# Thirty-two bytes less padding in front of the working tiles of a two-layer encoder

## The chip, the cores and the metric

The kernel runs on one core of one Trainium2 chip. It is one launch. The metric is the device time of one execution, in microseconds; the time of a kernel is the median of its runs. The core has a matrix engine (PE, with its weight loads shown apart as PEld), a vector engine (DVE), an activation engine (ACT), GpSimd (POOL) and a queue engine (SP) that issues most of the transfers. All of them work on SBUF, 128 partitions of on-chip memory; a tile takes the same byte addresses in each partition, so "address" below means the byte within a partition.

## The reference, cut to what matters

A trunk of two layers on x of 512 tokens by 1024 features, all in float32:

```
for l in range(2):
    h = rmsnorm(x, attn_norm[l])
    proj = h @ w_in[l]                       # 1024 -> 3072
    sb_out = stick_breaking_attention(...)   # 8 heads of 64
    df_out = differential_attention(...)     # 4 heads, two maps of 64 each, then a norm
    x = x + concat(sb_out, df_out) @ w_o[l]  # 1024 -> 1024
    h = rmsnorm(x, mlp_norm[l])
    u = square(relu(h @ w_ff1[l]))           # 1024 -> 4096
    x = x + u @ w_ff2[l]                     # 4096 -> 1024
return rmsnorm(x, final_norm)
```

## The kernel before, in words

**Three products for one.** Every large matrix product is made from operands split in two: a value is rounded to the type float32r (the "hi" part, by ACT in L109 or L233), and the rest is the value minus that (the "lo" part, by DVE in L125 or L234). The helper `three` (L284 to L289) then issues three matmuls into the same accumulator: hi by hi (L287), then the first operand's hi by the second's lo (L288), then lo by hi (L289). Two of three in a row use the same stationary operand. A matmul has a *stationary* operand (128 by 128, loaded into the array by a weight load) and a *moving* operand (up to 512 columns that stream past it). In profile rows the names stand as `out<-moving,stationary`.

**The stages of a layer.** First come the projections. The query and key blocks (outputs named `p`, with a head name such as `p0s1q`) have a weight block as the stationary operand (`whi`, `wlo`) and the 512 tokens of the normalised input as the moving one (`h_hi`, `h_lo`). The value blocks (`p0u`, `p0w` and so on, L427 to L429) are the other way round: 128 tokens of `h_hi` or `h_lo` are stationary and 256 columns of weights move. Attention (scores `S`, transposes `T`, values `O`) is interleaved by hand with the projections and with the first half of the output projection (`wo<-mdh`, `wo<-mdl`). The second half of it (`wo<-vdh`, `wo<-vdl`) runs alone. Then the MLP runs in four groups. Each has eight blocks `f` of 24 matmuls (stationary `whi`/`wlo`, moving `h_hi`/`h_lo`), and then 168 matmuls of the second MLP product in chains `X`, `V` and `Y`, which use seven products where eight would be plain; there the split activations `Ah`/`Al` are stationary and the weights `whi`/`wlo` move, 512 columns at a time.

**What sets the order.** Each engine executes its instructions in the order written out; `behind` adds ordering edges, and a small planner with a running clock decides between which projection steps an attention step is put. Weights arrive by transfer in `raw` tiles (SP queue) or `q` tiles (SP, and POOL for the ones added in the transfer), are split into `whi`/`wlo`, and are used by PE one or two units later.

**Where tiles lie.** Tiles take SBUF in the order in which pools and tiles are declared, each rounded up to 32 bytes. The pool `cp` (opened in L165) is first, behind 2,176 bytes that the program reserves. It holds, in this order: `lead` (a tile that nothing reads, 128 bytes), `begin`, `x`, `h_hi`, `h_lo`, `ssq`, `rbc`, `cos_t`, `sin_t`, `edge`, then small constants of 4 to 96 bytes (`lam_sm` to `fin`), and last `trail` (L230), a tile that nothing reads. Behind `cp` come the pools for `raw`, for `whi`/`wlo`, and all the pools of attention and of the MLP (`md*`, `v*`, `x*`, `z*`, `st*`, `kl*`, `hl*`, `y*`, `q*`, `F`, `Ah`, `Al`). All of these start one after another, and are multiples of 512 bytes long, but for a few small ones and the tiles `C` at the end of the attention pools.

So `x` begins at byte 3,072, which is 6 times 512; `h_hi` at 19,456, `h_lo` at 35,840, and `ssq` to `edge` at 52,224 to 60,416: all multiples of 512. `raw` begins at byte 63,008, which is 123 times 512 and 32 more, and so do all large tiles behind it: `whi` at 75,296, `wlo` at 83,488, `mdh` at 91,680, `vdh` at 124,448, the first `Ah` at 140,832, the second pair of `whi` in the MLP at 198,176, each 32 bytes past a multiple of 512. PE reads slices of these tiles at offsets that are multiples of 512 bytes (but for the single columns that `rms_b` spreads), so the remainder of a tile is the remainder of every operand that PE takes from it.

The lines that carry it:

```
    cp.tile([P, 32], F32, tag="lead", name="lead")
    begin = cp.tile([P, 192], F32, tag="begin", name="begin")
...
    fin = cp.tile([P, 24], F32, tag="fin", name="fin")
    cp.tile([P, 32], F32, tag="trail", name="trail")
```

Of the kernel before, what the change touches and what calls it, by code (L numbers as in the profile page):

```python
# [9 lines left out]
F32 = mybir.dt.float32  # L10
# [7 lines left out]
P = 128  # L18
# [144 lines left out]
def trunk(ctx, tc, opened, xT, w, w2, gfin, lamv, cos, sin, out):  # L163
    nc = tc.nc
    cp = ctx.enter_context(tc.tile_pool(name="cp", bufs=1))  # L165
# [61 lines left out]
    mean = cp.tile([P, 4], F32, tag="mean", name="mean")  # L227
    r2 = cp.tile([P, 4], F32, tag="r2", name="r2")
    fin = cp.tile([P, 24], F32, tag="fin", name="fin")
    cp.tile([P, 32], F32, tag="trail", name="trail")  # L230

    def split(hi, lo, src):
        a = nc.scalar.activation(hi, src, AF.Copy)  # L233
# [925 lines left out]
```

## Time and profile before

| | |
|---|---|
| time, median of 3 runs | 1157.63 us (1157.55 to 1157.69) |
| time of the profiled execution | 1158.41 us |
| its span | 1156.5 us |
| PE busy | 1146.8 us, 99% of the span, 5749 matmuls |
| weight loads busy | 964.4 us, 83% |
| DVE, ACT, POOL busy | 811.3, 642.3, 141.2 us |
| transfers | 166.47 MB |

The span is the time from the first instruction to the last; the profiled execution's own time is 1.9 us longer than its span. Matmuls overlap in the records: one of 512 columns is recorded as some 390 ns long, while the next begins some 230 ns after it. So the recorded duration is not what a matmul costs; the distance from one start to the next is. In a stretch in which PE runs without a gap that distance is the length of the stretch divided by the number of matmuls in it.

### The profile page before, as it was taken

How to read it: one execution, taken by the hardware profiler on the slowest of the kernel's cores; microseconds unless marked ns; L12 is line 12 of the kernel's file. 1: busy time of each engine (PE TensorE's matmuls, PEld its weight loads, DVE VectorE, ACT ScalarE, POOL GpSimd, SP SyncE). 2: the span in 40 equal slices, each digit the busy share in tenths (PEclk: the TensorE clock that was granted, in tenths of full speed). 3: DMA queues.
4: the chain of work that ended last, by engine and by line, in shares of the span. 5: the costliest groups of instructions: out<-in, count | busy, mean ns of one | idle time of the engine just before them, and what ended most of it. 6: DMA issues, size and time to landing. Idle time of an engine off the chain costs nothing.

```text
span 1156.5 us, 15843 instructions
## 1 busy us (share of the span) xinstructions
PE 1146.8 (99%) x5749; PEld 964.4 (83%) x5749; DVE 811.3 (70%) x1313; ACT 642.3 (56%) x1147; POOL 141.2 (12%) x225
## 2 busy tenths in 40 slices
PE   9999999999999999999999999999999999999997
PEld 7899889888888888888888998988888888888886
DVE  7898788775645746746778977887657467466476
ACT  6456666656646445455445665765574454553554
POOL 1000333100101101001000013330011010010010
PEclk9999999999999999999999999999999999999999
DMA  7564453266754845835226744522748459358162
GB/s 250 156 196 141 112 158 94 73 210 154 187 176 83 216 141 90 244 120 95 89 73 188 196 110 145 148 72 74 253 93 218 147 91 243 121 93 253 40 122 94
DMA packets 55853, 166.47 MB, mean 144 GB/s; under 512 B 6880, under 2 KB 8160, under 8 KB 55776
## 3 DMA queue, kind: packets, MB, share of 16 engines
q1 hardware_dynamic: 46128, 131.36, 35.8%
q0 software_dynamic: 9216, 33.56, 17.1%
q8 instruction: 45, 0.74, 0.3%
q10 hardware_dynamic: 432, 0.56, 0.1%
q14 instruction: 32, 0.26, 0.1%
HBM read 138.18 MB, written 2.10 MB: 121 GB/s over the span
## 4 chain that ended last, share of the span: by engine, by line
PE 96%; DVE 1%; DMA 1%; ACT 1%; issue 1%; POOL 0%; POOLq 0%; DVEq 0%; ACTq 0%
PE f L287 10%; PE f L288 10%; PE f L289 10%; PE X L287 5%; PE X L288 5%; PE X L289 5%; PE wo L287 3%; PE wo L288 3%; PE wo L289 3%; PE V L287 2%; PE V L289 2%; PE V L288 2%; PE Y L287 1%; PE Y L289 1%; PE Y L288 1%; PE T1s L606 1%
## 5 line engine op out<-in xcount | busy, mean ns | idle before, releaser
L125 DVE TENSOR_TENSOR wlo<-raw,whi 128x1024 fp32r<-128x1024 f32 (+1 forms) x130 | 154.2, 1189 | 113.7 <-ACT whi L109 111.7
L109 ACT ACTIVATE whi<-raw 128x1024 fp32r<-128x1024 f32 (+1 forms) x130 | 131.8, 1018 | 149.0 <-PE f L288 50.0
L287 PE MATMUL f<-h_hi,whi 128*128 128x512 f32 x512 | 202.9, 396 | 0.0
L109 ACT ACTIVATE whi<-q 128x512 fp32r<-128x512 f32 x224 | 129.9, 623 | 131.1 <-PE X L289 44.1
L288 PE MATMUL f<-h_lo,whi 128*128 128x512 f32 x512 | 202.5, 395 | 0.0
L289 PE MATMUL f<-h_hi,wlo 128*128 128x512 f32 x512 | 202.5, 395 | 0.0
L125 DVE TENSOR_TENSOR wlo<-q,whi 128x512 fp32r<-128x512 f32 x224 | 145.3, 687 | 78.6 <-ACT whi L109 74.2
L289 PEld LDWEIGHTS f<-h_hi,wlo 128*128 128x128 f32 x512 | 96.2, 188 | 23.3
L287 PEld LDWEIGHTS f<-h_hi,whi 128*128 128x128 f32 x512 | 96.2, 188 | 23.0
L288 PEld LDWEIGHTS f<-h_lo,whi 128*128 128x128 f32 x512 | 96.2, 188 | 23.0
L234 DVE TENSOR_TENSOR Al<-F,Ah 128x256 fp32r<-128x256 f32 (+2 forms) x96 | 74.7, 779 | 45.8 <-ACT Ah L233 45.8
L287 PE MATMUL X<-whi,Ah 128*128 128x512 f32 x248 | 96.9, 391 | 0.0
L288 PE MATMUL X<-wlo,Ah 128*128 128x512 f32 x248 | 96.6, 389 | 0.0
L289 PE MATMUL X<-whi,Al 128*128 128x512 f32 x248 | 96.5, 389 | 0.0
L233 ACT ACTIVATE Ah<-F 128x256 fp32r<-128x256 f32 (+2 forms) x96 | 67.6, 704 | 49.9 <-DVE F L892 48.1
L856 POOL DMA_DIRECT2D q<-in_w x48 | 41.9, 873 | 434.2 <-DVE wlo L125 386.0
L289 PEld LDWEIGHTS X<-whi,Al 128*128 128x128 f32 x248 | 46.5, 188 | 9.8
L287 PEld LDWEIGHTS X<-whi,Ah 128*128 128x128 f32 x248 | 46.6, 188 | 9.6
L288 PEld LDWEIGHTS X<-wlo,Ah 128*128 128x128 f32 x248 | 46.5, 188 | 9.6
L287 PE MATMUL V<-whi,Ah 128*128 128x512 f32 x128 | 49.8, 389 | 0.0
L288 PE MATMUL V<-wlo,Ah 128*128 128x512 f32 x128 | 49.8, 389 | 0.0
L289 PE MATMUL V<-whi,Al 128*128 128x512 f32 x128 | 49.8, 389 | 0.0
(658 smaller groups left out, 2557.8 us busy)
## 6 DMA issues: line engine op xcount, KB each, us to landing
raw<-in_w SPq DMA_DIRECT2D x126, 512.0 KB, 3.6
q<-in_w SPq DMA_DIRECT2D x64, 512.0 KB, 5.8
q<-in_w POOLq DMA_DIRECT2D x64, 512.0 KB, 5.5
x<-in_xT SPq DMA_DIRECT2D x8, 256.0 KB, 4.6
out_xT<-y SPq DMA_DIRECT2D x6, 256.0 KB, 2.2
raw<-in_w SPq DMA_DIRECT2D x6, 128.0 KB, 4.2
cos_t<-in_cos SPq DMA_DIRECT2D x2, 256.0 KB, 5.0
sin_t<-in_sin SPq DMA_DIRECT2D x2, 256.0 KB, 4.9
```

The costliest lines, as they stand in the source:

```text
L109: return self.nc.scalar.activation(o, src, AF.Copy)
L125: self.last = h, nc.vector.tensor_tensor(out=lo[:, a:b], in0=raw[:, a:b], in1=hi[:, a:b].bitcast(F32), op=ALU.subtract)
L233: a = nc.scalar.activation(hi, src, AF.Copy)
L234: nc.vector.tensor_tensor(out=lo, in0=src, in1=hi.bitcast(F32), op=ALU.subtract)
L287: nc.tensor.matmul(pt, ah, bh, start=first, stop=False, skip_group_check=goes_on)
L288: nc.tensor.matmul(pt, ah, bl, start=False, stop=False, skip_group_check=goes_on)
L289: nc.tensor.matmul(pt, al, bh, start=False, stop=last, skip_group_check=goes_on)
L606: nc.tensor.transpose(pt[:, off : off + P], u["w"][qi][:, kb * P : (kb + 1) * P], ident)
L856: nc.gpsimd.dma_start(t, quad(g, q, c), accum_op=ALU.add)
```

## The change

The pad `trail` at the end of `cp` is 24 floats long in place of 32, that is 96 bytes in place of 128. Nothing in `cp` before it moves. Everything behind it begins 32 bytes earlier: `raw` at 62,976, which is 123 times 512, `whi` at 75,264, and so on. With that, all large tiles begin at multiples of 512 bytes, except the two tiles `C` of the attention (2,052 bytes each), which lie behind small ones and move by the same 32 bytes. No instruction is added, removed or put in another place, on any engine, and no shape changes.

```diff
     fin = cp.tile([P, 24], F32, tag="fin", name="fin")
-    cp.tile([P, 32], F32, tag="trail", name="trail")
+    cp.tile([P, 24], F32, tag="trail", name="trail")
```

## The prediction

> **What bounds the kernel now.** I read the page first, then who PE waited for, then PE's busy time by stretches, and last single starts.
>
> ```profile
> span 1156.5 us, 15843 instructions
> PE 1146.8 (99%) x5749; PEld 964.4 (83%) x5749; DVE 811.3 (70%) x1313; ACT 642.3 (56%) x1147; POOL 141.2 (12%) x225
> PEclk9999999999999999999999999999999999999999
> PE 96%; DVE 1%; DMA 1%; ACT 1%; issue 1%; POOL 0%; POOLq 0%; DVEq 0%; ACTq 0%
> ```
>
> ```profile
> PE warm L217 <- POOL edge L211: 1.4, 1, 1.4
> PE S0s L519 <- DMA kl0s1k<-hl0s1q: 0.5, 1, 0.5
> ```
>
> PE is busy for 99% of the span at the full granted clock, 96% of the chain that ended last is PE, and in the whole execution it waits 1.9 us for others. Nothing that shortens a transfer or another engine can bring more than a few microseconds. The time is the sum of what matmuls cost one after another; the question is whether a matmul costs the same at other addresses.
>
> ```profile
> 0.00:20.00 20.00, 18.57 (x80) 13.64 (x81) 13.42 (x28) 15.94 (x29) 1.44 (x11) 1.00 0.85 292
> 325.00:369.80 44.80, 44.80 (x194) 36.06 (x192) 21.29 (x30) 24.49 (x38) 2.62 (x3) 1.00 0.43 110
> 369.80:407.90 38.10, 38.10 (x169) 31.54 (x168) 29.10 (x43) 18.31 (x29) 4.38 (x5) 1.00 0.80 212
> 580.00:813.00 233.00, 232.89 (x1387) 205.00 (x1385) 189.85 (x332) 138.44 (x286) 40.53 (x73) 1.00 0.44 127
> ```
>
> The columns after a stretch's length are busy time and number of PE, PEld, DVE, ACT and POOL, then clock, DMA share and GB/s. The second stretch is the eight `f` blocks of one MLP group, the third the group's `X`, `V` and `Y`. Both are gapless, with 512 columns per matmul and the same pattern of three. By the weight loads that start in each, 44.80 / 192 = 233.3 ns per matmul, and 38.10 / 168 = 226.8 ns. The same work costs 6.5 ns more in `f`. The starts show that it is steady:
>
> ```profile
> 516.01 0.40 PE L287 MATMUL f<-h_hi,whi 128*128 128x512 f32 x1
> 516.24 0.40 PE L288 MATMUL f<-h_lo,whi 128*128 128x512 f32 x1
> 516.48 0.40 PE L289 MATMUL f<-h_hi,wlo 128*128 128x512 f32 x1
> 516.71 0.40 PE L287 MATMUL f<-h_hi,whi 128*128 128x512 f32 x1
> ...
> 541.08 0.39 PE L287 MATMUL V<-whi,Ah 128*128 128x512 f32 x1
> 541.30 0.39 PE L288 MATMUL V<-wlo,Ah 128*128 128x512 f32 x1
> 541.53 0.39 PE L289 MATMUL V<-whi,Al 128*128 128x512 f32 x1
> 541.76 0.39 PE L287 MATMUL V<-whi,Ah 128*128 128x512 f32 x1
> ```
>
> What differs is which tiles are read. In `f` the moving operand lies at a multiple of 512 bytes and the stationary one 32 bytes past one; I write this (0, 32). In `X`, `V`, `Y` both lie 32 past: (32, 32). The costliest groups by form allow a test, since a recorded duration follows the distance (6 ns between `f` and `X`):
>
> ```profile
> L287 PE MATMUL f<-h_hi,whi 128*128 128x512 f32 x512 | 202.9, 396 | 0.0
> L289 PE MATMUL f<-h_hi,wlo 128*128 128x512 f32 x512 | 202.5, 395 | 0.0
> L288 PE MATMUL X<-wlo,Ah 128*128 128x512 f32 x248 | 96.6, 389 | 0.0
> L289 PE MATMUL V<-whi,Al 128*128 128x512 f32 x128 | 49.8, 389 | 0.0
> L288 PE MATMUL wo<-mdl,whi 128*128 128x512 f32 x64 | 25.2, 393 | 0.0
> L289 PE MATMUL wo<-mdh,wlo 128*128 128x512 f32 x64 | 25.1, 392 | 0.0
> L289 PE MATMUL wo<-vdh,wlo 128*128 128x512 f32 x64 | 24.9, 389 | 0.0
> L289 PE MATMUL Y<-whi,Al 128*128 128x512 f32 x64 | 24.9, 389 | 0.0
> L428 PE MATMUL p0u<-wlo,h_hi 128*128 128x256 f32 x64 | 17.9, 279 | 0.0
> L606 PE MATMUL T0s<-edge,sig0s 128*128 128x128 f32 x80 | 11.3, 272 | 0.0
> L289 PE MATMUL p<-h_hi,wlo 128*128 128x512 f32 x28 | 11.1, 396 | 0.0
> L918 PE MATMUL xT<-edge,x 128*128 128x128 f32 x32 | 4.1, 272 | 0.0
> L630 PE MATMUL O0s<-zl,vs 128*128 128x256 f32 x16 | 4.1, 281 | 0.0
> ```
>
> `wo<-vdh` has the same stationary tiles as `f` (`whi`, `wlo`), but a moving tile at 32: 389, like `X`, not like `f`. So neither the stationary tile nor the stage makes `f` slow; the moving one does, alone or by its distance from the stationary one. `wo<-mdh` is (32, 32) too, but cut up by attention steps: 392 to 393, between the two.
>
> **The change part by part.** It moves every tile behind the pad by 32 bytes: (32, 32) becomes (0, 0), (0, 32) becomes (0, 0), and so does (32, 0), the case of the value projections. No instruction, wait or queue moves. I take the reading that the *difference* of the two remainders counts, because two streams that read one memory side by side meet or miss each other by their distance, and a shift of both alike leaves that as it was. No row shows a 512-column product at (0, 0), so this is a choice, and both ends are kept below.
>
> `f`: 2 layers × 4 groups × 192 = 1536 matmuls (three rows of x512), from 233.3 to 226.8 ns: 1536 × 6.5 = −10.0 us, all on the path, since PE has no gap there. The cover holds: in the `f` stretch DVE and ACT are busy 21.29 and 24.49 us of 44.80, which becomes 43.5.
>
> Query and key projections `p`: 32 units × 24 = 768 matmuls, also (0, 32) now, most of them cut up by attention. Bounds: 0, and 768 × 6.5 = 5.0 us. The nearest row for a cut-up (0, 0) is `wo<-mdh,wlo` with 392 to 393, against 396 for `p`: 3 ns, so 768 × 3 = −2.3 us.
>
> Value projections, 16 units of 48 matmuls with 256 columns, 768 in all: (32, 0) to (0, 0). The last blocks of the kernel have 256 columns at (32, 32):
>
> ```profile
> L288 PE MATMUL Z<-wlo,Ah 128*128 128x256 f32 x4 | 1.1, 283 | 0.0
> ```
>
> 283 against 279 gives 768 × 4 = +3.1 us as one end. The other is half of what 512 columns gain, 768 × 3.3 = −2.5 us, in case they behave alike. The cut-up `O0s<-zl,vs` with 281 lies nearest in kind, as these products too are cut up by attention: 768 × 2 = +1.5 us.
>
> `X`, `V`, `Y`, both halves of `wo`, the scores and `O`: (32, 32) to (0, 0), nothing by this reading. Transposes: `T0s` reads a stationary tile at 32 and `xT` one at 0, both 272 ns: nothing. DVE and ACT could only matter where they are late for PE; in the attention stretch DVE is busy 189.85 of 233 us and PE 232.89, so there is no place where a few ns per instruction would come out. Transfers write other addresses, but PE's waits for them sum to 0.5 us. In the first 20 us PE is idle for 1.43 us and DMA at 0.85; whatever the loads gain there is bounded by that 1.43.
>
> Sum: −10.0 − 2.3 + 1.5 = −10.8 us. Against the profiled execution's own time (1158.41: the span and 1.9 us around it) that gives 1147.6; this execution is 0.8 us above the median of the runs, so for the median 1157.63 − 10.8 = 1146.8 us. This reading's own range: from −10.0 − 5.0 − 2.5 = −17.5 to −10.0 + 3.1 = −6.9, that is 1140 to 1151.
>
> **The rivals.** *A moving operand at a multiple of 512 is slow whatever the stationary one is.* Then `f` and `p` stay, and 744 `X`, 384 `V`, 192 `Y` and 192 `wo<-vdh` matmuls go from 226.8 to 233.3: 1512 × 6.5 = +9.8; 192 cut-up `wo<-mdh` by 3 ns give +0.6, the value projections between 0 and +2.5. It ends at 1168 to 1171 us, slower. For it: each 512-column group with moving 0 is slow and each with 32 fast, without exception. Against it: that 0 should be worse by itself than 32 needs a reason which nothing here shows. It decides from the first (0, 0) product at 233 in `X`.
>
> *Each operand has its own price.* From 256 columns, a stationary operand at 0 saves 4 ns (279 against 283); from 512, a moving one at 0 costs 6.5. Then (0, 0) lies between, at 233.3 − 4 = 229.3: `f` and `p` gain 2304 × 4 = 9.2 us, the 1512 lose 1512 × 2.5 = 3.8, the 192 cut-up some 0.5, and the value projections lose half of 6.5 on 768, 2.5 us. Net −2.4 us, 1155.2, at the edge of no change.
>
> *Addresses do nothing.* Then `f` is slow for another reason, say where `h_hi` and `h_lo` lie in the memory at large, and the time stays at 1157.6. For it speaks that the transposes do not care about 0 or 32. Against: `p` takes its weights only from the tiles at 75,296 and on, `f` also from those at 198,176, and both have 395 to 396; nothing else that I find separates `f` from `wo<-vdh`.
>
> The Trainium skill, page "SBUF — State Buffer", section "Who interferes with whom", gives PE two independent read ports, one for the moving operand and one for weight loads, and says that PE never waits on anyone; by that rule the change does nothing. Two steady rates for the same form at a clock of 1.00 and without a wait are not what the rule leads one to expect, so I give it little.
>
> **How the numbers follow.** A measurement of this kernel tells about 0.2%, 2.3 us, from no change. The distance reading: 0.54, at 1146.8. The moving operand alone: 0.30, at 1168 to 1171. Own prices: 0.08, at 1155.2, on the border, counted half as faster and half as the same. No effect: 0.08. So faster 0.58, same 0.12, slower 0.30. The range goes from 1141 to 1169: it holds the first case but for its lowest end, both middle ones, and the lower part of the slow one.
>
> **What would show it.** Right: in the profile after, the `f` rows have 389 to 390 ns and the `f` stretch 226.8 ns per matmul, with `X`, `V`, `Y` and `wo<-vdh` still at 389. `Z` and `p0u` rows show 281 to 283. The moving-alone reading shows as 395 in the `X`, `V` and `Y` rows with `f` unchanged; own prices as some 392 in both; no effect as no row changed. The prediction would also be wrong if (0, 0) were no like of (32, 32) at all, so that both stages leave 227 and 233, or if weights came late for the faster `f` blocks, to be seen as waits of PE for DVE or DMA.

## The result, and the profile after

The changed kernel takes 1146.82 us, median of 4 runs (1146.63 to 1147.08), against 1157.66 before (4 runs, 1157.55 to 1157.84). The ratio is 0.9906, with a 95% interval of 0.9889 to 0.9924: faster by 10.8 us, 0.9%. The profiled execution took 1146.63 us with a span of 1144.7. The profiled execution of the kernel before was 0.8 us above its median, so the two traces differ by more than the medians do: 11.8 us in the span.

The page of the changed kernel, its answer on whom PE waited for, and PE's busy time by stretches (columns as in the stretches of the prediction; the second stretch is again one group's `f` blocks, the third its `X`, `V` and `Y`):

```profile
span 1144.7 us, 15843 instructions
PE 1135.8 (99%) x5749; PEld 967.2 (84%) x5749; DVE 811.4 (71%) x1313; ACT 641.1 (56%) x1147; POOL 141.0 (12%) x225
PEclk9999999999999999999999999999999999999999
PE 98%; DVE 1%; issue 1%; ACT 0%; POOL 0%; POOLq 0%; DVEq 0%; ACTq 0%
```

```profile
PE warm L217 <- POOL edge L211: 1.4, 1, 1.4
```

```profile
0.00:20.00 20.00, 18.64 (x83) 14.15 (x84) 13.80 (x28) 16.01 (x29) 1.43 (x11) 1.00 0.85 302
322.45:365.97 43.52, 43.52 (x194) 36.07 (x193) 21.27 (x30) 24.32 (x38) 2.62 (x3) 1.00 0.41 108
365.97:404.05 38.08, 38.08 (x170) 31.56 (x169) 29.12 (x43) 18.32 (x29) 4.38 (x5) 1.00 0.80 200
```

PE is as busy as before, at the same clock, with less to do: 11.0 us less busy time for the same 5749 matmuls. The `f` stretch now starts and ends with a block and is 43.52 us long; with 192 matmuls that is 226.7 ns for one (233.3 before). The third stretch is 38.08 us for 168, 226.7, as before (38.10). Both DVE and ACT are as busy in the `f` stretch as they were, and PE still does not wait for them.

Groups by form, costliest first (busy us, mean ns of one):

```profile
L287 PE MATMUL f<-h_hi,whi 128*128 128x512 f32 x512 | 199.9, 390 | 0.0
L289 PE MATMUL f<-h_hi,wlo 128*128 128x512 f32 x512 | 199.6, 390 | 0.0
L288 PE MATMUL X<-wlo,Ah 128*128 128x512 f32 x248 | 96.6, 390 | 0.0
L289 PE MATMUL V<-whi,Al 128*128 128x512 f32 x128 | 49.9, 390 | 0.0
L289 PE MATMUL wo<-mdh,wlo 128*128 128x512 f32 x64 | 25.1, 393 | 0.0
L289 PE MATMUL wo<-vdh,wlo 128*128 128x512 f32 x64 | 24.9, 390 | 0.0
L428 PE MATMUL p0u<-wlo,h_hi 128*128 128x256 f32 x64 | 18.1, 283 | 0.0
L606 PE MATMUL T0s<-edge,sig0s 128*128 128x128 f32 x80 | 11.3, 272 | 0.0
L289 PE MATMUL p<-h_hi,wlo 128*128 128x512 f32 x28 | 11.0, 392 | 0.0
L630 PE MATMUL O0s<-zl,vs 128*128 128x256 f32 x16 | 4.2, 282 | 0.0
```

`f` went from 395 and 396 to 390, `p` from 396 to 392, the value projections rose from 279 to 283, and all else in these rows stands within 1 ns of where it stood. Summing the distances from each matmul's start to the next one's, over all 5749 of each trace and by kind, gives the account:

```
                              before    after   difference (us)
f            (1536 matmuls)   358.78   348.81   -9.97
p, 512 wide  (768)            182.34   180.21   -2.13
value proj., 256 wide (768)    91.31    93.22   +1.92
scores S     (256)             42.09    41.30   -0.80
X, V, Y, wo, transposes, O and the rest         -0.60
sum of all                                      -11.58
```

Of the scores' 0.80, 0.5 us is the one wait of PE for a transfer that the trace before had (`S0s L519`) and this one has not. The change does not explain it: two versions below that are as slow as the kernel before have no such wait either, and their scores sum to 41.39 and 41.29 us. Sums from single traces also differ by up to a microsecond from the start of the kernel alone: in the traces of this study the first value product begins 16.2 to 17.3 us after the first instruction.

### The profile page after: what moved, and what is told of

Its sections match the earlier page's. It is cut to its first block, busy times and chain, and to the rows that moved or that the text cites. A ratio compares the mean times of both kernels' runs of the same rounds, so it can differ in the third digit from the quotient of the medians.

```text
span 1144.7 us, 15843 instructions
## 1 busy us (share of the span) xinstructions
PE 1135.8 (99%) x5749; PEld 967.2 (84%) x5749; DVE 811.4 (71%) x1313; ACT 641.1 (56%) x1147; POOL 141.0 (12%) x225
## 4 chain that ended last, share of the span: by engine, by line
PE 98%; DVE 1%; issue 1%; ACT 0%; POOL 0%; POOLq 0%; DVEq 0%; ACTq 0%
PE f L287 10%; PE f L288 10%; PE f L289 10%; PE X L288 5%; PE X L287 5%; PE X L289 5%; PE wo L287 3%; PE wo L289 3%; PE wo L288 3%; PE V L288 2%; PE V L289 2%; PE V L287 2%; PE Y L289 1%; PE Y L287 1%; PE Y L288 1%; PE T1s L606 1%
## 5 line engine op out<-in xcount | busy, mean ns | idle before, releaser
L287 PE MATMUL f<-h_hi,whi 128*128 128x512 f32 x512 | 199.9, 390 | 0.0
L289 PE MATMUL f<-h_hi,wlo 128*128 128x512 f32 x512 | 199.6, 390 | 0.0
L288 PE MATMUL f<-h_lo,whi 128*128 128x512 f32 x512 | 199.5, 390 | 0.0
```

The costliest lines, as they stand in the source:

```text
L287: nc.tensor.matmul(pt, ah, bh, start=first, stop=False, skip_group_check=goes_on)
L288: nc.tensor.matmul(pt, ah, bl, start=False, stop=False, skip_group_check=goes_on)
L289: nc.tensor.matmul(pt, al, bh, start=False, stop=last, skip_group_check=goes_on)
```

## The experiments

My theory was that the time of a matmul depends on the distance between the addresses of its moving and its stationary operand. The rivals were a price for each operand by itself, an advantage of multiples of 512 as such, and traffic of other engines. In what follows (m, s) are the remainders of the moving and the stationary operand. A cycle stands for 1/2.4 ns, the unit in which the steady distances at equal offsets come out whole (226.67 ns is 544, 120.0 is 288).

**Single groups, PE alone.** The kernel is two tiles at multiples of 512 and this loop, with N = 24:

```diff
+for wd, m, s in cases():
+    pt = ps.tile([P, 512], F32, tag="t", name=f"w{wd}m{m}s{s}x")
+    for n in range(N):
+        nc.tensor.matmul(pt[:, 0:wd], sta[:, s // 4 : s // 4 + P], mov[:, m // 4 : m // 4 + wd],
+                         start=n == 0, stop=n == N - 1)
```

> Nothing of the trunk is computed here: the kernel only runs groups of 24 equal matmuls on two tiles that begin at multiples of 512, one group for each pair of byte offsets (moving, stationary) out of 0, 16, 32, 48, 64, 96, 128, 256, at 512 and at 256 columns, and a few at 384 and 128. No other engine works beside them. Distance reading: groups with equal offsets give 226.7 ns per matmul of 512 columns wherever they lie, (0, 32) gives 233.3, and 256 columns give 120 at equal offsets and 116.7 at (32, 0). If distances repeat after 64 bytes, (0, 64), (0, 128) and (0, 256) give 226.7 too. Rival, a price for each operand alone: the time of a pair is a term of the moving offset and one of the stationary one, so that (0, 0) plus (32, 32) equals (0, 32) plus (32, 0) in each width. Rival, traffic of other engines: with PE alone all pairs give the same, and the 6.5 ns of the kernel come from DVE, ACT or transfers that meet PE at certain addresses.

Measured, from the groups by form (the name holds width, moving and stationary offset):

```profile
L45 PE MATMUL w512m32s0x<-mov,sta 128*128 128x512 f32 x24 | 5.8, 395 | 0.0
L45 PE MATMUL w512m0s64x<-mov,sta 128*128 128x512 f32 x24 | 5.8, 395 | 0.0
L45 PE MATMUL w512m0s32x<-mov,sta 128*128 128x512 f32 x24 | 5.8, 395 | 0.0
L45 PE MATMUL w512m64s64x<-mov,sta 128*128 128x512 f32 x24 | 5.6, 390 | 0.0
L45 PE MATMUL w512m32s32x<-mov,sta 128*128 128x512 f32 x24 | 5.6, 389 | 0.0
L45 PE MATMUL w256m32s32x<-mov,sta 128*128 128x256 f32 x24 | 3.0, 283 | 0.0
L45 PE MATMUL w256m32s0x<-mov,sta 128*128 128x256 f32 x24 | 3.0, 279 | 0.0
L45 PE MATMUL w256m0s64x<-mov,sta 128*128 128x256 f32 x24 | 2.9, 276 | 0.0
```

The mean distances of starts from the fifth matmul of a group on, in cycles, are 544.0 at (32, 32) and 543.9 at (64, 64), (128, 128) and (256, 256). They are 560.2 at (0, 32), 560.1 at (32, 0), 559.7 at (0, 64), 558.1 at (0, 128) and 544.0 at (0, 256). With 256 columns they are 288 at equal offsets, 280.2 at (32, 0) and 272.0 at (64, 0).

Traffic of other engines is out: PE alone shows the kernel's very numbers. A price for each operand is out: (32, 32) and (64, 64) sum to 1088, (32, 64) and (64, 32) to 1120. A period of 64 bytes, which I had as a possibility, is out, and 256 fits.

At 512 columns equal offsets are alike at all multiples of 32 that I tried; (96, 96) has 545.4 and settles at 544 within the group. They are not alike where the offset is 16 past a multiple of 32: (16, 16) has 554.8 cycles and (48, 48) 560.0, while (16, 48) and (48, 64) have 544. So the rule "same remainder, fast" holds only for offsets that are multiples of 32 bytes, which is what the kernel has. Nor does the distance alone say how slow an unequal pair is: (64, 0) and (128, 64) have 549 to 550 cycles, (0, 64) and (96, 32) have 560.

**All large tiles 32 bytes past.**

```diff
-    cp.tile([P, 32], F32, tag="lead", name="lead")
+    cp.tile([P, 40], F32, tag="lead", name="lead")
```

> The pad at the front is 32 bytes longer, so that all large tiles, x and h among them, begin 32 bytes past multiples of 512: every product is at (32, 32). Distance reading: as the changed kernel, 1146.8 us, f stretch 226.8 ns per matmul. Rival, the multiple of 512 is what helps: f and the other products fall to some value of their own, 1150 us or more.

1146.55 us (1146.44 to 1147.21), ratio to the kernel before 0.9908 [0.9892, 0.9925]: as fast as the changed kernel, with no large tile at a multiple of 512.

```profile
L287 PE MATMUL f<-h_hi,whi 128*128 128x512 f32 x512 | 199.7, 390 | 0.0
```

So the multiple of 512 is not what helps; what helps is that the two operands agree.

**x and h 32 past, the rest at multiples of 512.** The same `lead` and

```diff
-    cp.tile([P, 24], F32, tag="trail", name="trail")
+    cp.tile([P, 16], F32, tag="trail", name="trail")
```

> x and h begin 32 past, all tiles behind the pad at multiples of 512: f and p at (32, 0), value projections at (0, 32), X, V, Y and wo at (0, 0). Distance reading without a sign: as the kernel before, f 233.3 ns, 1157.6 us. With a sign, that is if stationary 32 ahead of moving is not the same as 32 behind: f anywhere from 220 to 233 ns, 1137 to 1158 us; the value products at (32, 0), 280 of 288 cycles, speak for a gain. Own prices, 0 good for the stationary operand and 32 good for the moving one: f below 226.8, less than 1146 us.

1158.67 us (1158.19 to 1159.30), ratio 1.0010 [1.0001, 1.0020]. Its `f` stretch and group:

```profile
324.58:369.38 44.80, 44.80 (x193) 36.00 (x192) 21.30 (x30) 24.50 (x38) 2.62 (x3) 1.00 0.43 108
L287 PE MATMUL f<-h_hi,whi 128*128 128x512 f32 x512 | 202.7, 396 | 0.0
```

The gain is gone: 44.80 / 192 = 233.3 ns, with the moving operand 32 ahead as with the stationary one. The kernel before took 1157.50 us on this chip, 1.2 us less; 1.0 of it shows in the value projections, now at (0, 32): their start distances sum to 92.28 us against 91.31.

**The rest 64 past.**

```diff
-    cp.tile([P, 24], F32, tag="trail", name="trail")
+    cp.tile([P, 40], F32, tag="trail", name="trail")
```

> The pad is 64 bytes longer than in the changed kernel: x and h at 0, all tiles behind the pad 64 past a multiple of 512. Distance reading with a period of 64 bytes: as the changed kernel, 1146.8 us, f 226.8. With a period of 128 or more: f at another value, between 220 and 240 ns, 1137 to 1168 us.

1157.76 us (1157.32 to 1158.03), ratio 1.0002 [0.9993, 1.0011]: 64 bytes apart, with the stationary operand of `f` ahead, is as slow as 32.

```profile
324.41:369.21 44.80, 44.80 (x193) 35.92 (x192) 21.31 (x30) 24.49 (x38) 2.62 (x3) 1.00 0.42 110
```

**The rest 256 past,** with the pad at 88 floats:

> The pad is 256 bytes longer than in the changed kernel: f, p and value products have their operands 256 bytes apart, all others are at equal offsets. Distance reading with a period of 256 bytes, as the single groups had it (544 cycles at (0, 256), and 558 at (0, 128)): as the changed kernel, 1146.8 us, f stretch 226.8 ns. Rival, only tiles at multiples of 512 go together: as the kernel before, 1157.6 us, f 233.3.

1146.97 us (1146.28 to 1147.35), ratio 0.9905 [0.9888, 0.9921]: 256 bytes apart is as good as none.

```profile
L287 PE MATMUL f<-h_hi,whi 128*128 128x512 f32 x512 | 199.9, 390 | 0.0
```

**Finer groups, in the kernel's pattern of three.** As the first kernel, with two moving and two stationary tiles taken in turn and distances in steps of 16 bytes, other widths, and bf16.

> Nothing of the trunk is computed here. Groups of 36 matmuls in the kernel's own pattern of three (two moving tiles, two stationary tiles, all at multiples of 512), with PE alone. Distance reading with a period of 256 bytes: at 512 columns only distances 0 and 256, 512, 768 give 226.7 ns, all others 229 to 234, and a group at moving 256 and stationary 256 - d is the mirror of one at moving 0 and stationary d; at 256 columns a distance of 64 gives 113.3 ns and 0 gives 120. If it is the weight load that takes cycles from the moving stream, the extra at distance 0 is the same number of cycles at 192, 256, 320, 384, 448 and 512 columns (32 cycles, 13.3 ns). Rival, a number for each column: the extra grows with the columns. For 2-byte operands I have no forecast: if the meeting is one of reads of 16 bytes, twice as many columns per read should make it weaker, 213 to 220 ns at 512 columns with a spread below 6 ns.

Mean distance of starts in ns at moving 0, by stationary offset (some offsets left out):

```
columns   0      16     32     48     64     96     128    192    224    240    256
512       226.7  226.6  233.3  233.3  233.3  234.3  233.3  228.9  233.3  226.7  226.7
256       120.0  118.3  118.3  117.8  113.3  118.8  118.7  117.8  116.7  120.0  120.0
512 bf16  215.8  215.8  215.8  -      215.8  -      215.8  -      -      -      215.8
```

```profile
L57 PE MATMUL xw512m0s128x<-mov,sta 128*128 128x512 f32 x36 | 8.6, 395 | 0.0
L57 PE MATMUL xw512m0s64x<-mov,sta 128*128 128x512 f32 x36 | 8.6, 396 | 0.0
L57 PE MATMUL xw512m256s192x<-mov,sta 128*128 128x512 f32 x36 | 8.4, 392 | 0.0
L57 PE MATMUL xw512m0s256x<-mov,sta 128*128 128x512 f32 x36 | 8.3, 389 | 0.0
L57 PE MATMUL hw512m0s0x<-half,half 128*128 128x512 bf16 x36 | 7.9, 380 | 0.0
L57 PE MATMUL hw512m0s32x<-half,half 128*128 128x512 bf16 x36 | 7.9, 379 | 0.0
```

At 512 columns 0, 256, 512 and 768 give 544 cycles, and all else from 32 to 224 bytes gives 549 to 563; 4, 8 and 12 bytes give 558, 554 and 560. A distance of 16 bytes is good too in three of four cases, but at moving 256 and stationary 16 it gave 233.3, where the first kernel had 226.7 for the same pair. The mirror that I had forecast fails: (0, 64) gives 233.3 and (256, 192) gives 228.9, so it matters which operand is ahead. A shift of the moving operand by 256 bytes changes neither: (256, 64) gives 233.3 too, and (0, 192) 228.9. That is what a period of 256 says.

The loss belongs to wide matmuls. At 448 columns the four distances tried (0, 32, 64 and 128 bytes) lie within 6 cycles; at 384 columns 32 bytes apart is as good as 0 (416 cycles) and 128 costs 7 more; at 320 and 192 columns the distance does nothing.

The extra over the columns at distance 0 is 32 cycles at 256, 320, 384 and 512 columns, so there it is paid per matmul and not per column; at 448 it is 38, and at 192 columns the matmul takes 268 cycles whatever the distance. My forecast of one number for all widths held for four of six. The bf16 groups have no trace of the effect: 518 cycles at every distance. The Trainium skill, page "TensorE: Matmul & The Clock Gate", section "Back-to-back issue gap", gives 518 cycles for 512 columns of an isolated matmul, and some 131 ns for a sustained stream of them. The bf16 groups, which are a stream, agree with the first (215.8 ns); no float32r group reaches it, and nothing here reaches the second.

At 256 columns remainders alone do not fix the steady value. 64 bytes apart gave 113.3 ns at (0, 64) and 117.8 at (256, 192), and (256, 64) gave 113.3 in the first kernel and 117.8 here. In the whole kernel with the rest 64 past, value products with the same remainders ran at 113.3 ns in long stretches of `p0u` and at 117.8 in some of `p0w`. These cases differ in what ran before and also in the tiles that are read, and no run changes one of the two alone.

**Which load is it?** Groups in which each matmul's own pair agrees and the weight load beside it does not, and the reverse.

```diff
+m = 0 if kind in ("same", "none") else d * (n % 2)
+s = {"same": 0, "none": d, "own": d * (n % 2), "next": d * (1 - n % 2)}[kind]
```

> Nothing of the trunk is computed here. Groups of 48 matmuls with PE alone, for distances d of 32, 64 and 128 bytes. In the groups same all operands are at 0, in none all moving ones at 0 and all stationary ones at d. In own, every second matmul has both operands at d and the others both at 0, so that each is at an equal offset with its own weights, but the weight load that runs while it streams, that of the next matmul, is d away. In next it is the other way round: each matmul is d away from its own weights, and the load that runs beside it is at its own offset. If the moving stream meets the weight load of the next matmul: at 512 columns same and next 226.7 ns, own and none 233.3. If it is the matmul's own pair that counts: same and own 226.7, next and none 233.3. At 256 columns same gives 120 ns, and its fellow (next, or own) with it.

For 32, 64 and 128 bytes at 512 columns: same 226.7 throughout, none 233.3, 233.3 and 232.3, own 231.7, 231.8 and 228.3, next 230.0, 231.7 and 230.0 ns.

```profile
L46 PE MATMUL nonew512d32x<-mov,sta 128*128 128x512 f32 x48 | 11.4, 395 | 0.0
L46 PE MATMUL ownw512d32x<-mov,sta 128*128 128x512 f32 x48 | 11.3, 394 | 0.0
L46 PE MATMUL nextw512d32x<-mov,sta 128*128 128x512 f32 x48 | 11.2, 392 | 0.0
L46 PE MATMUL samew512d32x<-mov,sta 128*128 128x512 f32 x48 | 11.0, 389 | 0.0
```

Neither reading holds: both mixed kinds lie between. At 256 columns it is no clearer: same is 120.0 ns, and own and next lie between 116.7 and 120.0. The run does not settle which weight load the stream meets, its own or the next; that it is a weight load at all is not shown.

**A version that takes the one loss back.** The changed kernel lost 1.9 us in the value projections, whose 256 columns like a distance that 512 columns do not. The variants write the weights of 12 of 16 value units (576 matmuls) some bytes into their tiles; the first two units of each layer lie in other tiles and stay.

```diff
+            wide = 0 if k // 2 else 64
+            at = SHIFT if _UNITS[i][0] == "v" else 0
+            hi, lo = (self.pools[k // 2].tile([P, 1024 + wide], F32R, tag=t, name=f"{t}{i}")[:, at : at + 1024]
+                      for t in ("whi", "wlo"))
```

SHIFT is 8 floats, then 16; the last has 8 and also 64 bytes of pad in front of `xh`. Beside them, on the same chip, the changed kernel again.

> The changed kernel beside the three variants on one chip, so that a difference of a few tenths of a per cent can be read: 1146.8 us.

> The changed kernel with the weights of 12 of 16 value units written 32 bytes into their tiles (the tiles are 256 bytes longer, so that all else stays at distances that are multiples of 256): these 576 products of 256 columns are at (32, 0) again, all of 512 columns stay at equal offsets. Distance reading: 116.7 in place of 120 ns, 576 x 3.3 = -1.9 us, 1144.9 us. Rival, the value products are held by something else while attention is between them: no change, 1146.8.

> The same with 64 bytes. The single groups gave 113.3 ns at (64, 0) in one order and 117.8 in another, the whole kernel with a pad 64 bytes longer a mixture of 113 and 117 to 118: between 576 x 2.2 = -1.3 and 576 x 6.7 = -3.8 us, 1143.0 to 1145.5 us.

> As the variant with 32 bytes, and 64 bytes of pad in front of the tiles xh: the 224 value products of attention with 256 columns get moving operands 64 bytes from their stationary ones, 113.3 to 117.8 in place of 120 ns, at most 224 x 6.7 = -1.5 us more; scores keep equal offsets among themselves. 1143.4 to 1144.9 us.

```
changed kernel             1147.13 (1147.03 to 1147.24)   ratio to before 0.9908 [0.9893, 0.9923]
weights 32 bytes in        1145.50 (1145.44 to 1145.75)                   0.9894 [0.9879, 0.9909]
weights 64 bytes in        1146.07 (1145.37 to 1146.40)                   0.9898 [0.9883, 0.9913]
32 bytes, and 64 for xh    1146.07 (1145.67 to 1146.55)                   0.9900 [0.9884, 0.9917]
```

With 32 bytes the time falls by 1.6 us, 0.14%; the runs of the two do not overlap, though the intervals of the ratios to the kernel before do. That is less than the 1.9 us forecast. The group is back where it was (line numbers are 3 higher there):

```profile
L431 PE MATMUL p0u<-wlo,h_hi 128*128 128x256 f32 x64 | 17.9, 279 | 0.0
L292 PE MATMUL f<-h_hi,wlo 128*128 128x512 f32 x512 | 199.3, 389 | 0.0
```

The traces do not put all of it down to the edit. The 576 shifted products sum to 68.33 us, against 69.54 in the changed kernel's trace beside it: 1.2 us less. Some 0.6 us lies in the start of the kernel, before the first value product (16.5 us after the first instruction against 17.2), where no shifted product has run; the trace of the changed kernel has a wait of 0.7 us of PE for ACT there, the variant's one of 0.3. The units that stay lose 0.3 us. So the shift is worth about 1.2 us, and the rest of the 1.6 is not shown to come from it.

64 bytes bring less than was expected of them (1146.07, expected 1143.0 to 1145.5), and the pad for `xh` brings nothing on top (1146.07, expected 1143.4 to 1144.9). The version with 32 bytes has the lowest median of the study.

## Why the prediction was right

**The sum.** Forecast 1146.8, measured 1146.82, with the gain of 10.8 us as summed. By the starts the three terms of the sum come to −10.2 us: `p` and the value projections together fell 0.6 short. Against the profiled execution the sum gave 1147.6, and it took 1146.63; where nothing had been priced 1.4 us were gained (scores 0.8, the rest 0.6), which covers the 0.6 and most of that 1 us more. 0.5 of it is the transfer wait that the change does not explain.

**`f`: right.** −10.0 forecast, −9.97 by the starts, 390 ns in the rows and 226.7 ns per matmul in the stretch. The choice between the difference of the remainders and the moving operand alone was the risk in it: `X`, `V`, `Y` and `wo<-vdh` at 390 decided it as the prediction said they would, and the single groups, the shift of everything by 32 bytes and the one by 256 bear it out.

**`p`: right.** −2.3 from the nearest row of cut-up matmuls, −2.13 by the starts; `p` now has 392, `wo<-mdh` 393.

**Value projections: right in sign, a little low.** +1.5 taken, +1.92 by the starts; the rows show 283, as the row of `Z`, the end of the range that I did not take.

**Everything at nothing.** `X`, `V`, `Y`, `wo`, `O` and the transposes moved by 0.2 us or less each; the scores gave 0.8, which no term had. The cover held: in the profiled execution no wait of PE on DVE, ACT or a transfer appeared, and another execution of the same kernel, the one beside the variants, has a single wait for ACT, 0.7 us at its start.

**The rivals.** The moving operand alone fell with the first `X` row. Own prices fell with it and with the sum of the four pairs. "Addresses do nothing" fell with `f`. The sentence of the Trainium skill behind it, page "SBUF — State Buffer", section "Who interferes with whom", that PE's two read ports are independent and PE never waits on anyone, is not enough for float32r operands: at 512 columns they take 226.7 or 233.3 ns by how the two operands lie to each other, with nothing but PE at work. That PE waits on no other engine is not touched by this, and that the two ports are what meets is not shown. The bf16 groups have the same time at every distance, which is what the sentence leads one to expect.

**Luck in it.** That the median is met to 0.02 us is luck: the terms were 0.6 us short, and gains that I had not priced filled the gap. The reason that I gave, two streams that meet or miss by their distance, made me say only that (0, 0) equals (32, 32), and no run shows which two reads meet. Its period I had nowhere; with the pad 64 bytes longer, a value as round to the eye, the kernel would have stayed where it was.

## What to carry to other kernels

Where a float32r kernel is bound by PE and its matmuls have 512 columns, compare the start distances of its stages: if one runs at 233 ns and another at 227, look at the addresses, and bring each moving tile to the same remainder modulo 256 bytes as the stationary tile it is multiplied with, both at multiples of 32. Equal remainders are what counts, wherever they lie, so one pad between two groups of tiles can do it, and a small constant added in front of them later can undo it. This is a rule for 512 columns: at 320 the distance did nothing, and 256 columns did better 32 bytes apart. So measure your own width in a kernel of single groups, which takes one run.

## What the runs showed that I had not expected

The period is 256 bytes: at 512 columns 0 and 256 bytes apart give 544 cycles, and 32 to 224 give 549 to 563. 64 bytes with the stationary operand ahead is no better than 32; with the moving one ahead it cost 5 to 16 cycles, by the pair. At equal offsets float32r still pays 32 cycles per matmul at 256, 320, 384 and 512 columns, while bf16 pays 6 at 256 and 512 columns, at every distance. And the remainders are not the whole story: at 256 columns and 64 bytes apart the same pair ran at 113.3 or at 117.8 ns in different kernels. Which of PE's reads meet, what else decides at 256 columns, why 16 bytes apart is good in some pairs and bad in others, and why equal offsets of 16 or 48 bytes are slow, stays open.
